# Sums of squares from row-major copies on ScalarE, query projections ahead of the first keys and values, stores on ScalarE's queue, and the memory's norm ahead of the prompt attention

## The chip, the cores and the metric

The kernel runs on one core of a Trainium2 chip. The metric is the device time of one execution in microseconds (us); of several executions the median is given. TensorE is called PE, VectorE DVE, ScalarE ACT, GpSimd POOL and SyncE SP. The kernel is written in a tile framework: its scheduler puts the instructions of each engine in a fixed order, and each engine then works through its own order, waiting where an operand or a buffer isn't ready.

## What is computed

One step of a decoder layer on a prompt of 512 tokens and 8 single sample tokens, all in fp32 with D = 1024. Cut to what matters here:

```python
def rmsnorm(x, g):
    return x * lax.rsqrt(jnp.mean(x * x, axis=-1, keepdims=True) + EPS) * g

def mixer_inputs(x, g_mix, w_in):
    z = rmsnorm(x, g_mix) @ w_in
    return u, q, kv, gates

def mem_project(mem, g_mem, w_xkv):
    return rmsnorm(mem, g_mem) @ w_xkv

def decoder_layer(h, ...):
    u, q, kv, gates = mixer_inputs(h, g_mix, w_in)
    y = concat(pool_mix(u), nsa(q, kv, gates))
    h = h + y @ w_out
    h = h + cross_attn(rmsnorm(h, g_xattn), mem_kv)
    return h + conv_ffn(rmsnorm(h, g_ffn))
```

`nsa` is attention with three branches (compressed blocks, selected blocks, a window) and gates; the sample tokens attend to a paged cache of keys and values. `pool_mix` takes trailing means of 2, 4, 8 or 16 positions minus the token, times a matrix per group. `mem_kv` are keys and values of 256 memory tokens.

## The kernel before

**Data and products.** Activations lie transposed, channels on the partitions: eight blocks (k = 0 to 7) of 128 channels by 520 tokens, in two halves of 260 columns. Each fp32 operand of a projection is split into a rounded high part and the rest (`split`, lines 124 to 129: ACT copies the high part, DVE subtracts), and three products (high x high, high x low, low x high) are added in PSUM. A projection tile of 128 output channels (`project`, line 204) is therefore 8 x 3 x 2 = 48 matmuls of 260 columns. Weights come by DMA into a ring of two buffers ("w_raw"); `split_w` turns them into `w_hi` (ACT, line 117) and `w_lo` (DVE, line 120), two buffers each. Since the weight has to be split before the first product of its tile, ACT's and DVE's order decides when PE may begin a tile.

**The norm.** The products use x times its gain (`xn_hi`, `xn_lo`), and the factor 1/rms of a token is multiplied in afterwards, when the result leaves PSUM (`R1`, `R1n`). Tokens lie along the columns, so the sum of squares over channels is one over partitions: `x_block` (346 to 358) squares each block (six on ACT, two on POOL), POOL and DVE add the squares up in two accumulators, and `token_sums` (from 246) adds over the partitions by small products with a column of ones (lines 255 and 257). `rstd_from` (L213 to L227) is a chain of 13 small DVE operations, `spread_rstd` (L233 to L239) transposes it by PE and copies it to `R`.

**The front.** A few products with a zero tile (L315) come first. Then the first two tiles of keys and values (`ps_kv0`) are projected together, block by block as x arrives. Query tile 0 follows in two banks of its own (`ps_q0`). Then `merge(kv_first, q_tiles)` interleaves two streams by the costs that they yield: `kv_first` multiplies the first keys and values by R1 into `ztile` (a ring of three), stores them (`O["kv_t"]`, L464, SP's queue), rearranges them into `xp_raw` and compresses them by eight small products per tile (L580), then transposes (L595, L478). `q_tiles` projects query tiles 1 to 3 and copies each into `Qst`, `Qbd` and `Qe`. The weights of query tiles 2 and 3 (`load_in` in `q_tiles`) are asked for after the stores. The gate tile (L541) with `turn_queries` (L611) comes next, then `kv_tiles(1)` with the scores of the cached keys (`cached_scores`, L628, L635), then `kv_tiles(2)` and nine steps of `pooling` with `sample_back`, then `sample_attention` with 18 more steps of `pooling`.

**Cached keys.** `fetch_keys` brings one sample's eight pages: of even samples by gathers from POOL (L333), of odd ones by SP (L331), 128 KB each.

**The seam.** After the sample tokens' attention the last steps of `pooling` (the rest of its projection and, for each of four groups, U, POOL's adds in `pl_s`, `pl_d` (L938) and a product with `wpl` (L954) that is split into `y_hi` and `y_lo`) run beside `split_keys`. Then PSUM is given out anew (`ps2`, `ps3`), and `merge(prompt_attention, beside)` starts: `prompt_attention` makes scores (L1002), masked and raised to powers by DVE and ACT (L1008, L1010), transposes (L1031) and weighted sums; `beside` runs `memory` (from 1094), which splits the memory tokens into `mT_hi` and `mT_lo`, squares them on ACT, adds the squares on POOL (`accm`, L1106), sums by ones (L1112), takes rstd, transposes it (L1118), and then projects the memory's keys and values (L1132).

## Time and profile before

| | |
|---|---|
| median of 3 runs | 899.33 us (898.23 to 901.22) |
| the profiled execution | 901.21 us, span 899.1 us |
| mean granted TensorE clock | 0.974 of full speed |
| PE busy | 857.2 us (95%) |
| weight loads (PEld) | 789.3 us (88%) |
| DVE busy | 567.5 us (63%) |
| ACT busy | 369.6 us (41%) |
| POOL busy | 121.6 us (14%) |
| moved by DMA | 122.84 MB, 137 GB/s mean |
| chain of waits | PE 85%, DVE 6%, DMA 4%, ACT 2% |

The busy time is the time of an engine with an instruction in it; a matmul at a low clock is busy as well, only longer. The chain of waits follows the last instruction back to whatever released it. 2.1 us of the profiled execution's time lie outside the span.

### The profile page before, as it was taken

The numbers are of one execution on the slowest core, as the hardware profiler recorded it, in microseconds if no ns is written. First come the engines' busy times: TensorE is split into PE (matmuls) and PEld (weight loads), VectorE is DVE, ScalarE is ACT, GpSimd is POOL, SyncE is SP. The second block draws the span as 40 slices with busy tenths as digits, with TensorE's granted clock in tenths as the row PEclk, the third lists the DMA queues.
The fourth block names the chain that finished last, engine by engine and source line by source line (L and its number), as shares of the span: only waits on it lengthen the run. The fifth ranks groups of instructions, "written<-read, shape, count | busy, mean of one in ns | idle before, by whom it ended". The sixth has DMA issues, their size and how long they took to land.

```text
span 899.1 us, 17462 instructions
## 1 busy us (share of the span) xinstructions
PE 857.2 (95%) x7085; PEld 789.3 (88%) x7085; DVE 567.5 (63%) x1450; ACT 369.6 (41%) x684; POOL 121.6 (14%) x114
## 2 busy tenths in 40 slices
PE   7989999699999999999999999999999999999993
PEld 6978786587777789999889999999999999999993
DVE  6653173987665767788764578773377774367734
ACT  5432132566656546344343254441144442134541
POOL 6713033400000004000043000000000000000132
PEclk9988999979999999999999999999999999999995
DMA  8943795342332146477514643322333322332212
GB/s 281 322 153 107 269 354 199 117 154 97 106 118 71 47 132 213 143 236 250 179 47 118 230 137 98 94 93 83 87 84 85 90 94 94 95 94 84 81 36 95
DMA packets 108175, 122.84 MB, mean 137 GB/s; under 512 B 4592, under 2 KB 95088, under 8 KB 106032
## 3 DMA queue, kind: packets, MB, share of 16 engines
q1 hardware_dynamic: 103488, 100.79, 35.5%
q0 software_dynamic: 3600, 19.55, 5.9%
q10 hardware_dynamic: 1008, 1.40, 0.4%
q8 instruction: 55, 0.90, 0.4%
q14 instruction: 24, 0.20, 0.1%
HBM read 114.58 MB, written 10.69 MB: 139 GB/s over the span
## 4 chain that ended last, share of the span: by engine, by line
PE 85%; DVE 6%; DMA 4%; ACT 2%; issue 1%; SPq 0%; DVEq 0%; ACTq 0%; POOL 0%; POOLq 0%
PE ps_pp L204 56%; PE ps_tb L1132 3%; PE ps_sc L1002 3%; DMA w_u<-in_w_up_dram 3%; PE ps_o L1038 2%; PE ps_tb L1153 2%; PE ps_tb L973 2%; PE ps_tf L1031 2%; PE ps_pp L1604 2%; DVE w_lo L120 1%; PE ps_x L1322 1%; PE ps_x L1341 1%; ACT w_hi L117 1%; PE ps_s L1379 1%; DMA w_kv<-in_w_in_t_dram 1%
## 5 line engine op out<-in xcount | busy, mean ns | idle before, releaser
L204 PE MATMUL ps_pp<-x_hi,w_lo 128*128 128x260 f32 x832 | 169.2, 284 | 0.5 <-DVE w_lo L120 0.5
L204 PE MATMUL ps_pp<-x_hi,w_hi 128*128 128x260 f32 x832 | 169.5, 284 | 0.1
L204 PE MATMUL ps_pp<-x_lo,w_hi 128*128 128x260 f32 x832 | 167.8, 283 | 0.0
L204 PEld LDWEIGHTS ps_pp<-x_hi,w_lo 128*128 128x128 f32 x832 | 128.7, 188 | 1.2 <-DVE w_lo L120 0.7
L204 PEld LDWEIGHTS ps_pp<-x_hi,w_hi 128*128 128x128 f32 x832 | 128.7, 188 | 0.5 <-ACT w_hi L117 0.3
L204 PEld LDWEIGHTS ps_pp<-x_lo,w_hi 128*128 128x128 f32 x832 | 128.1, 188 | 0.4 <-issue 0.4
L117 ACT ACTIVATE w_hi<-w_raw 128x1024 fp32r<-128x1024 f32 (+1 forms) x52 | 54.2, 1043 | 107.6 <-PE ps_pp L204 85.9
L120 DVE TENSOR_TENSOR hT<-hT,ps_pp 128x520 f32<-128x520 f32 (+1 forms) x44 | 28.4, 646 | 88.6 <-PE ps_pp L204 74.5
L117 ACT ACTIVATE w_hi<-w_u 128x1024 fp32r<-128x1024 f32 x44 | 46.7, 1061 | 76.0 <-PE ps_pp L204 65.0
L120 DVE TENSOR_TENSOR w_lo<-w_raw,w_hi 128x1024 fp32r<-128x1024 f32 (+1 forms) x52 | 64.5, 1241 | 4.3 <-ACT w_hi L117 4.0
L204 PE MATMUL ps_pp<-h_lo,w_hi 128*128 128x260 f32 x304 | 61.3, 283 | 0.0
L204 PE MATMUL ps_pp<-h_hi,w_hi 128*128 128x260 f32 x304 | 61.2, 282 | 0.0
L204 PE MATMUL ps_pp<-h_hi,w_lo 128*128 128x260 f32 x304 | 61.1, 282 | 0.0
L120 DVE TENSOR_TENSOR ext<-ps_pp,R 128x512 f32<-128x512 f32 x44 | 30.4, 690 | 45.4 <-PE ps_pp L204 45.3
L120 DVE TENSOR_TENSOR w_lo<-w_u,w_hi 128x1024 fp32r<-128x1024 f32 x44 | 53.9, 1226 | 7.0 <-ACT w_hi L117 6.7
L204 PE MATMUL ps_pp<-xn_hi,w_hi 128*128 128x260 f32 x208 | 48.8, 316 | 5.0 <-ACT w_hi L117 2.9
L1551 POOL DMA_DIRECT2D out_ffn_t_dram<-last x1 | 0.6, 574 | 351.1 <-DVE last L114 351.1
L204 PE MATMUL ps_pp<-xn_lo,w_hi 128*128 128x260 f32 x208 | 46.5, 304 | 0.8 <-DVE xn_lo L129 0.7
L204 PEld LDWEIGHTS ps_pp<-h_hi,w_hi 128*128 128x128 f32 x304 | 46.9, 188 | 0.2 <-ACT h_hi L117 0.2
L204 PEld LDWEIGHTS ps_pp<-h_hi,w_lo 128*128 128x128 f32 x304 | 46.9, 188 | 0.0
L204 PEld LDWEIGHTS ps_pp<-h_lo,w_hi 128*128 128x128 f32 x304 | 46.8, 188 | 0.0
L204 PE MATMUL ps_pp<-xn_hi,w_lo 128*128 128x260 f32 x208 | 45.7, 302 | 0.3 <-DVE w_lo L120 0.3
(457 smaller groups left out, 1884.3 us busy)
## 6 DMA issues: line engine op xcount, KB each, us to landing
w_u<-in_w_up_dram SPq DMA_DIRECT2D x44, 512.0 KB, 4.6
xkr<-in_cache_mem_dram SPq DMA_DIRECT2D x16, 512.0 KB, 5.1
xvr<-in_cache_mem_dram SPq DMA_DIRECT2D x16, 512.0 KB, 6.2
w_raw<-in_w_down_dram SPq DMA_DIRECT2D x8, 1024.0 KB, 5.2
Kt<-in_k_t_dram SPq DMA_DIRECT2D x32, 128.0 KB, 4.0
w_raw<-in_w_in_t_dram SPq DMA_DIRECT2D x8, 512.0 KB, 4.3
w_raw<-in_w_xkv_dram SPq DMA_DIRECT2D x4, 1024.0 KB, 5.4
w_v<-in_w_xkv_dram SPq DMA_DIRECT2D x4, 1024.0 KB, 5.1
```

Source lines behind the costliest of these rows:

```text
L117: act.activation(o, i, AF.Copy, scale=scale)
L120: (eng or dve).tensor_tensor(o, a, b, op=op)
L204: pe.matmul(o, a[:, k, :], x[:, hf, :], start=(k == 0 and j == 0), stop=(k == kt - 1 and j == 2))
L973: pe.matmul(ps[:, :HT], a[:, k, :], y[x][:, k, hf, :], start=(k + j == 0), stop=(k == 3 and j == 2))
L1002: pe.matmul(ss_[hl][:, 0:c0 + nk], Qst[:, h, qc], k[:, g, u, 0:c0 + nk], start=(u == 0), stop=(u == 1))
L1031: pe.transpose(pt[:, hh * P:(hh + 1) * P], pr[hh][:, kb * P:(kb + 1) * P], ident)
L1038: pe.matmul(po[hp * 64:(hp + 1) * 64, g * 256:(g + 1) * 256], Vtok[:, br, kb - 1, g * 64:(g + 1) * 64], pTs[kb - 1][:, hp * 256:(hp + 1) * ...
L1132: pe.matmul(ps[:, 0:MEM], a[:, k, :], x[:, k, :], start=(k == 0 and j == 0), stop=(k == 7 and j == 2))
L1153: pe.matmul(ps[i], x[:, k, ts_], w[:, kl, :], start=(k == 0 and j == 0), stop=(k == KT - 1 and j == 2))
L1322: pe.matmul(s[:, ql * MEM:(ql + 1) * MEM], a[:, 2 * h + dh, hf, ql * P:(ql + 1) * P], x[:, 2 * h + dh, :], start=(n == 0), stop=(n == 5))
L1341: pe.matmul(po, v[:, mb, dh * P:(dh + 1) * P], x[:, mb, :], start=(mb + j == 0), stop=(mb + j == 3))
L1604: pe.matmul(ps[:, l, :HT], a[:, dl, k, :], x[:, hf, :], start=(k + j == 0), stop=(k == kt - 1 and j == 2))
```

## The change

It does five things. (1) The host gives x and the memory tokens a second time in their natural layout, tokens on the partitions (`x_row`, `x_row_s`, `mem_row`); ACT squares a row of 1024 channels and sums it in the same instruction (`accum_out`), one for each 128 tokens. The squares of the transposed blocks, their sums on POOL and DVE and the products with ones go. (2) There are 16 products with the zero tile where there were 6. (3) The query tiles run alone, directly after tile 0; `kv_begin` makes the first keys' two `ztile`s ahead of them; compression, gate and `turn_queries` are merged after them; the weights of query tiles 2 and 3 and some keys are fetched earlier; the sample's first scores and the window's scores run beside `kv_tiles(1)`, and all 27 steps of `pooling` are beside `sample_attention`. (4) The stores of keys and values go out on ACT's queue. (5) `memory_norm` takes the memory's rstd before `sample_attention`; `memory` keeps the splits and the projections. The two sides of PSUM after the seam are exchanged, and one bank of the prompt attention is taken earlier.

```diff
-    for i in range(6):
+    for i in range(10):
         pe.matmul(pw, warm[:, 0:P], warm, start=True, stop=True)
...
     def x_block(k):
         split(xn_hi[:, k], xn_lo[:, k], hT[:, k], scale=vec[:, k:k + 1])
-        if k == 0:
-            act.activation(accs[k], hT[:, k], AF.Square)
...
-    raw_q0 = load_in(4, "w_q")
+    raw_q0 = ptile(wp, [P, 2, KT, P], "w_raw", bufs=2, name="w_q")
+    sp.dma_start(raw_q0[:, 0], w_in[4])
+    for i in range(NQB):
+        sp.dma_start(xrow[:, i], A["x_row"][i])
+    sp.dma_start(xrow_s, A["x_row_s"])
+    sp.dma_start(raw_q0[:, 1], w_in[5])
...
+        if k == 1:
+            for _ in range(6):
+                pe.matmul(pw, warm[:, 0:P], warm, start=True, stop=True)
...
     w = split_w(raw_q0[:, 0])
+    ss1 = ptile(rp, [P, 8], "ss", bufs=2)
+    dve.memset(ss1, float(D))
+    for i in range(NQB + 1):
+        n = P if i < NQB else NB
+        act.activation(ptile(px0, [P, D], "xsq")[0:n], xrow[:, i] if i < NQB else xrow_s, AF.Square,
+                       accum_out=ss1[0:n, i:i + 1])
     with tc.high_priority():
-        rs1 = rstd_from(token_sums(bank("s"), *accs), 5)
+        rs1 = rstd_from(ss1[:, 0:5], 5)
...
+    raw_q1 = load_in(6, "w_q")
+    fetch_keys(2)
+    fetch_keys(3)
     wc_raw = ptile(wp, [P, 2, 8, 2, 64], "w_raw", bufs=2, name="wc_raw")
     for c in range(2):
         sp.dma_start(wc_raw[:, c], A["w_cmp_t"][:, c])
-    fetch_keys(2)
-    fetch_keys(3)
+    fetch_keys(4)
+    fetch_keys(5)
...
+    def kv_begin():
+        for c in range(2):
+            z0.append(ztile())
+            tt(z0[c], ps_kv0[c][:, :, :HT], R1, OP.mult)
...
-            sp.dma_start(O["kv_t"][c], z)
+            act.dma_start(O["kv_t"][c], z)
...
-            sp.dma_start(O["kv_t"][2 * br + c], z)
+            act.dma_start(O["kv_t"][2 * br + c], z)
...
+    def sample_front():
+        yield from cached_scores(0)
+        fetch_keys(7)
+        fetch_window_keys()
+        fetch_window_values(0)
+        yield 3.0
+        yield from window_scores()
...
+        pos[2] = bank("o")
...
+    def memory_norm():
+        mrow = ptile(wp, [P, 2, D], "w_raw", bufs=2, name="mrow")
+        sp.dma_start(mrow, A["mem_row"])
+        ssm = ptile(rp, [P, 8], "ss", bufs=2)
+        for i in range(2):
+            act.activation(ptile(pb, [P, D], "wv", name="msq"), mrow[:, i], AF.Square, accum_out=ssm[:, i:i + 1])
+        vcopy(rsm, rstd_from(ssm[:, 0:2], 2))
+        ps = bank("tb")
+        for i in range(2):
+            pe.transpose(ps[:, i * P:(i + 1) * P], rsm[:, i:i + 1].to_broadcast([P, P]), ident)
+        acopy(Rm, ps[:, 0:MEM])
...
-    merge((kv_first(), 10.8), (q_tiles(), 17.0))
-    gates = gate_tile()
-    merge((gates, 4.0), (turn_queries(), 3.0))
+    kv_begin()
+    run(q_tiles())
+    w_g = ptile(p0, [P, KT, 24], "w_g")
+    sp.dma_start(w_g, A["w_gate_t"])
+    raw_kv = [load_in(10)]
+    merge((kv_first(), 4.0), (gate_tile(w_g), 4.0), (turn_queries(), 3.0))
+    raw_kv.append(load_in(12))
     fetch_keys(6)
-    merge((kv_tiles(1), 12.0), (cached_scores(0, 4.0), 10.0))
...
-    merge((ahead(), 18.0), (sample_back(), 24.0))
+    merge((kv_tiles(1, raw_kv[0]), 12.0), (sample_front(), 12.0))
+    merge((kv_tiles(2, raw_kv[1]), 12.0), (sample_back(), 12.0))
...
-    merge((sample_attention(), 20.0), ((next(pools) for _ in range(18)), 12.0))
+    memory_norm()
+    pools = pooling()
+    merge((sample_attention(), 20.0), ((next(pools) for _ in range(27)), 19.0))
...
-    es_ps2 = open_psum("ps2", "right", tb=3)
-    es_ps3 = open_psum("ps3", "left", sc=2, tf=2, o=1)
+    es_ps2 = open_psum("ps2", "left", tb=3)
+    es_ps3 = open_psum("ps3", "right", o=1, sc=2, tf=2)
```

The scheduler puts all 16 zero products first on PE. Its order on ACT changes most at the front. Before, from the last block of x to the weights of query tile 2 (`xn_hi` and `sqx` belong to x, `w_q` are the query weights, `xp_raw` and `Qst` the rearranged keys and the queries):

```order
L128 ACTIVATE xn_hi<-x_71,vec 128x520
L358 ACTIVATE sqx<-x_71 128x520
L117 ACTIVATE w_hi<-w_q 128x1024 x2
L117 ACTIVATE R<-ps_s 128x2x256 x2
L117 ACTIVATE xp_raw<-ztile 64x32x8 x4
L117 ACTIVATE Qst<-ztile 64x512 x2
L117 ACTIVATE pe_t<-ps_s 64x1
```

The same stretch of ACT after, from the last blocks of x:

```order
L128 ACTIVATE xn_hi<-x_71,vec 128x520 x4
L388 ACTIVATE xsq,ss<-xrow 128x1024 x3
L117 ACTIVATE w_hi<-w_q 128x1024
L388 ACTIVATE xsq,ss<-xrow 128x1024
L388 ACTIVATE xsq,ss<-xrow_s 8x1024
L117 ACTIVATE w_hi<-w_q 128x1024
L117 ACTIVATE R<-ps_s 128x2x256 x2
L479 DMA out_kv_t_dram<-ztile 128x520
L117 ACTIVATE xp_raw<-ztile 64x32x8 x2
L479 DMA out_kv_t_dram<-ztile 128x520
L117 ACTIVATE Qst<-ztile 64x512 x2
L117 ACTIVATE xp_raw<-ztile 64x32x8 x2
```

The squares now stand between the blocks of x and the weights of query tile 0, three ahead of its `w_hi`; the two rows that follow are `Qst` of tile 1 and only then `w_hi` of query tiles 2 and 3.

On PE the seam changes. Before (`accm` are the memory's sums, `ps_sc` scores of the prompt, `ps_tf` their transposes, the last three rows the first of the memory's projection):

```order
L954 MATMUL ps_pp<-pl_d,wpl 128x260 x8
L1002 MATMUL ps_sc<-Ksl,Qst 128x416 x4
L1112 MATMUL ps_tb<-ones,accm 128x1 x2
L1002 MATMUL ps_sc<-Ksl,Qst 128x416 x12
L1031 MATMUL ps_tf<-cst,prob 128x128 x8
L1002 MATMUL ps_sc<-Kwn,Qst 128x384 x2
L1118 MATMUL ps_tb<-cst,rs_y 128x128 x2
L1132 MATMUL ps_tb<-mT_hi,w_hi 128x256
L1132 MATMUL ps_tb<-mT_lo,w_hi 128x256
L1132 MATMUL ps_tb<-mT_hi,w_lo 128x256
```

After:

```order
L969 MATMUL ps_pp<-pl_d,wpl 128x260 x8
L1017 MATMUL ps_sc<-Ksl,Qst 128x416 x4
L1139 MATMUL ps_tb<-mT_hi,w_hi 128x256
L1139 MATMUL ps_tb<-mT_lo,w_hi 128x256
L1139 MATMUL ps_tb<-mT_hi,w_lo 128x256
```

The memory's projection follows directly on the first four scores; twelve scores, the transposes and the rest are spread through it, 24 projection products apart. Ahead of both pieces stand 40 products of the pooling's projection after the sample's last transposes (`oS`), where there were 30.

## Rows read from the trace of the kernel before

**Rows 1.** The page, busy time: us (share of the span) x instructions.

```profile
PE 857.2 (95%) x7085; PEld 789.3 (88%) x7085; DVE 567.5 (63%) x1450; ACT 369.6 (41%) x684; POOL 121.6 (14%) x114
```

**Rows 2.** Windows: length, busy us of each engine (x), TensorE clock, DMA share, GB/s.

```profile
20.00:30.00 10.00, 9.24 (x74) 8.57 (x74) 7.88 (x23) 2.01 (x2) 7.87 (x8) 1.00 0.93 304
...
71.00:78.00 7.00, 7.00 (x33) 6.53 (x32) 2.76 (x11) 0.92 (x3) 5.49 (x5) 0.52 0.57 200
...
161.00:189.60 28.60, 19.44 (x82) 14.93 (x80) 25.82 (x92) 15.53 (x39) 7.66 (x10) 0.78 0.48 150
...
600.00:700.00 100.00, 100.00 (x835) 100.00 (x834) 56.54 (x107) 32.27 (x42) 0.00 (x0) 1.00 0.34 96
```

**Rows 3.** PE's waits from 0 to 240 us: us in total, times, longest.

```profile
PE ps_pp L954 <- DVE y_lo L129: 2.9, 1, 2.9
...
PE ps_tb L595 <- DVE kcp L575: 2.4, 1, 2.4
...
PE ps_pp L954 <- DVE U L120: 1.9, 1, 1.9
...
PE ps_tb L1112 <- POOL accm L120: 2.1, 1, 2.1
...
PE ps_tb L812 <- DVE oS L114: 1.7, 1, 1.7
...
PE ps_tb L819 <- DVE Swn L857: 0.7, 1, 0.7
```

**Rows 4.** Timeline of PE, the front: start, us, instruction, count [idle before <-releaser].

```profile
23.33 1.62 PE L255 MATMUL ps_s<-ones,acc 128*128 128x1 f32 x14
...
26.88 0.40 PE L204 MATMUL ps_pp<-xn_hi,w_lo 128*128 128x260 f32 x2
...
35.15 0.40 PE L204 MATMUL ps_pp<-xn_hi,w_hi 128*128 128x260 f32 x2
...
42.66 1.90 PE L580 MATMUL ps_s<-xp_raw,wc_raw 128*128 128x66 f32 x16
...
49.58 0.80 PE L204 MATMUL ps_pp<-xn_hi,w_hi 128*128 128x260 f32 x2 [2.07 <-ACT w_hi L117]
...
53.99 0.40 PE L204 MATMUL ps_pp<-xn_hi,w_hi 128*128 128x260 f32 x2
...
63.12 0.40 PE L204 MATMUL ps_pp<-xn_hi,w_lo 128*128 128x260 f32 x2
```

**Rows 5.** Timeline of ACT, same columns.

```profile
8.86 0.63 ACT L117 ACTIVATE w_hi<-w_kv 128x512 fp32r<-128x512 f32 x1 [1.84 <-DMA w_kv<-in_w_in_t_dram]
...
36.10 1.28 ACT L117 ACTIVATE Qst<-ztile 64x512 fp32r<-64x512 f32 x2 [0.96 <-DVE ztile L120]
...
48.48 2.00 ACT L117 ACTIVATE w_hi<-w_q 128x1024 fp32r<-128x1024 f32 x2
...
126.34 1.16 ACT L719 ACTIVATE Ssl<-Ssl,mc 128x1025 f32<-128x1025 f32 x1 [1.47 <-DVE mc L718]
```

**Rows 6.** DMA view from 0 to 70 us: GB/s in 40 equal slices.

```profile
GB/s 0 260 346 273 393 411 399 414 249 181 289 183 234 269 309 391 351 298 283 300 295 395 373 352 310 254 277 411 288 14 220 376 293 0 9 0 5 0 0 0
```

**Rows 7.** Timeline of POOL's queue, a gather of keys.

```profile
18.15 1.42 POOL L333 DMA_INDIRECT Kt<-in_k_t_dram,ix_k  x1 [0.19 <-issue]
```

**Rows 8.** Timeline of DVE, the front and the seam.

```profile
27.50 1.22 DVE L120 TENSOR_TENSOR w_lo<-w_q,w_hi 128x1024 fp32r<-128x1024 f32 x1
...
161.78 0.69 DVE L938 SCALAR_TENSOR_TENSOR pl_d<-pl_s,U 128x512 f32<-128x512 f32 x1
...
170.76 1.21 DVE L938 SCALAR_TENSOR_TENSOR pl_d<-pl_s,U 128x512 f32<-128x512 f32 x1
```

**Rows 9.** Timeline of SP's queue, the first stores of keys.

```profile
32.36 0.95 SPq L464 DMA_DIRECT2D out_kv_t_dram<-ztile  x2
```

**Rows 10.** Timeline of PE, the seam.

```profile
166.65 1.04 PE L954 MATMUL ps_pp<-pl_d,wpl 128*128 128x260 f32 x4
...
173.57 3.59 PE L954 MATMUL ps_pp<-pl_d,wpl 128*128 128x260 f32 x8 [2.90 <-DVE y_lo L129]
```

More of the change, by code (lines that the diff above doesn't have):

```diff
@@ L153, in decoder_step @@
     hT = ptile(px0, [P, KT, 2, HT], "x0")
+    xrow = ptile(px0, [P, NQB, D], "xrow")
+    xrow_s = ptile(px0, [NB, D], "xrow_s")
     vec = const.tile([P, 76], F32, name="vec")
@@ L318, in decoder_step @@
     xs1 = blocks(xn_hi, xn_lo)
-    accs = [ptile(px0, [P, 2, HT], f"acc{i}") for i in range(2)]
     def row_numbers():
@@ L408, in decoder_step @@
     Vtok = ptile(at, [P, 2, NQB, P], "Vtok")
+    rsm = ptile(at, [P, 2], "rsm")
+    Rm = ptile(at, [P, MEM], "Rm")
     smp, es_smp = open_pool("smp")
@@ L454, in dup_split @@
         vcopy(lo[b], lo[a].bitcast(F32))
+    z0 = []
+    def kv_begin():
+        for c in range(2):
+            z0.append(ztile())
+            tt(z0[c], ps_kv0[c][:, :, :HT], R1, OP.mult)
     def kv_first():
-        z0 = [ztile(), ztile()]
-        for c in range(2):
-            tt(z0[c], ps_kv0[c][:, :, :HT], R1, OP.mult)
         for c in range(2):
             z = z0[c]
-            sp.dma_start(O["kv_t"][c], z)
+            act.dma_start(O["kv_t"][c], z)
             x = ptile(p0, [P, 528], "chg", bufs=2, name="xp_raw").rearrange("p (j x) -> p j x", j=8)
@@ L501, in q_tiles @@
         for j in range(2):
-            raw = raw_q0 if j == 0 else load_in(4 + 2 * j, "w_q")
-            if j == 1:
-                fetch_keys(4)
-                fetch_keys(5)
+            raw = (raw_q0, raw_q1)[j]
             for l in range(2):
@@ L1022, in weighted @@
         def weighted(qb, br, g, pr):
-            if br + g == 0:
+            if br + g == 0 and qb not in pos:
                 pos[qb] = bank("o")
@@ L1158, in memory @@
             pool.dma_start(mv_out[:, :, cs], Vx[:, :, cs])
-    merge((kv_first(), 10.8), (q_tiles(), 17.0))
-    gates = gate_tile()
-    merge((gates, 4.0), (turn_queries(), 3.0))
-    fetch_keys(6)
-    merge((kv_tiles(1), 12.0), (cached_scores(0, 4.0), 10.0))
-    fetch_keys(7)
-    fetch_window_keys()
-    fetch_window_values(0)
-    pools = pooling()
-    def ahead():
-        yield from kv_tiles(2)
-        for _ in range(9):
-            yield next(pools)
-    merge((ahead(), 18.0), (sample_back(), 24.0))
+    kv_begin()
[5 more added lines that the diff above has]
+    raw_kv.append(load_in(12))
+    fetch_keys(6)
+    merge((kv_tiles(1, raw_kv[0]), 12.0), (sample_front(), 12.0))
+    merge((kv_tiles(2, raw_kv[1]), 12.0), (sample_back(), 12.0))
     es_p0.close()
     pb, es_pb = open_pool("pb")
-    merge((sample_attention(), 20.0), ((next(pools) for _ in range(18)), 12.0))
+    memory_norm()
+    pools = pooling()
+    merge((sample_attention(), 20.0), ((next(pools) for _ in range(27)), 19.0))
     es_pb.close()
@@ L1635, in lay_out @@
     given["x_t"] = np.concatenate([xp, xs], axis=3)
+    given["x_row"] = x["x_prompt"][0].reshape(NQB, P, D)
+    given["x_row_s"] = x["x_sample"][:, 0]
+    given["mem_row"] = x["mem_prompt"][0].reshape(2, P, D).transpose(1, 0, 2)
     given["w_in_t"] = x["w_in"][0][:, :1792].reshape(KT, P, 14, P).transpose(2, 1, 0, 3)
```

49 lines of the change are left out of this document (8 added, 41 removed).

## The prediction

> **What bounds the kernel now.** I read the page's busy times first: PE is at work in 857.2 of 899.1 us, 95%, and no other engine is above 63% [rows 1]. In the middle of the program a window of 100 us has PE busy for all of it at full clock (1.00, the 2.4 GHz level) [rows 2]. So nothing is to be had there, and the change touches nothing behind the seam but order. What can be had is where PE waits, where it runs at the low clock level (1.2 GHz), and products that go. The windows say where: from 161.0 to 189.6 PE is busy 19.4 of 28.6 us at a mean clock of 0.78, and from 71 to 78 the clock is 0.52 with PE busy throughout [rows 2]. The list of PE's waits gives names, nearly all of them ACT's and DVE's chains at the front and the seam [rows 3]. The timeline gives the price of a product: from 53.99 to 63.12 are 76 of them, 0.12 us each; from 49.58 to 53.99, after two waits of 2.4 and 2.1 us, are 18, 0.245 each, so a fall of the level there costs 2.2 us [rows 3, 4].
>
> **The change, part by part** (times of the profiled execution, 901.2 us).
>
> *A. First keys and values, -7.0.* Before, they end at 27.2 (the last two products start at 26.88) [rows 4]. The second weights' first half lands at 8.86 and is split by 9.4 [rows 5]; 6 of 96 products can run ahead of that, and 90 x 0.12 = 10.8 then give 20.2. For that the level must be high from there: 16 zero products keep PE at work from 1.5 until about 8, where six left it idle before the first block. The products with ones, 14 of them in 1.62 us in one piece [rows 4], go; so do POOL's sums, beside which DVE's operations are longer. Bounds: -4 if the level comes as late as before (most of 28 products at twice the price, 3 us back), -8.5 if the waits within go too.
>
> *B. Query tile 0, +1.1.* It took 27.2 to 35.15 = 7.95 [rows 4]. Now its `w_hi` stands on ACT behind three squares of row-major x. The third row block is behind 2.1 MB of x, 1.05 of first weights, 0.5 of `w_q` and 1.6 of itself, 5.3 MB by the tiles' sizes; at 260 to 411 GB/s in the early slices, 304 from 20 to 30 us [rows 2, 6], I let it land at 19.5. One square 1.16 (priced by the nearest, an exponential of 1,025 elements with a sum), `w_hi` 1.0, `w_lo` 1.2 [rows 5, 8]: the second part of the first block runs at 22.9, then 44 products, 5.3, and the six small ones for R, 0.9: 29.2, or 9.0 after A's end. The other two squares and the rstd chain run beside this tile. Bounds 0 (rows land by 18) and +4 (by 22.3).
>
> *C. Query tiles 1 to 3, -1.0.* Before, 35.15 to 63.35 = 28.2, with 3.8 of compression in it (two pieces of 1.90 [rows 4]), which moves behind. The other 24.4 were 17.3 of products, two waits of 4.4, the 2.2 of low level and 0.5. Now tile 2's `w_hi` is queued on ACT behind both copies of tile 1's `Qst`, which wait for tile 1's end: `ztile` 0.7, `Qst` 1.28, `w_hi` 1.0 [rows 5, 8], and `w_lo` still 0.7 after the four products that don't need it; 3.9 in all. With the same fall of the level that saves 0.5, without it 2.7; I take 1.0, nearer the first, since the waits of before were about as long [rows 3]. The weights of tiles 2 and 3 are fetched ahead of most keys and should land by 36. The new query-first order leaves nothing beside these tiles to fill a wait.
>
> *D. Compression, turned queries and cached scores, +2.0.* They follow each other as small products with copies by ACT and DVE between, with only the gate's 32 products beside. A stretch of that kind stood at 0.52 from 71 to 78 and lost 3.3 us [rows 2]. Bounds 0 (this replaces that stretch) and +5.
>
> *E. Middle, +0.3.* The memory's norm puts two squares (1.16 each) on ACT and 14 small operations on DVE, and PE's transposes wait for them: I put 1.0, while the wait on `Swn`, 0.7 [rows 3], gets other work before it. Bounds 0 and +2.
>
> *F. Seam, -7.4.* 19.4 us busy at 0.78 is some 15.2 at full clock. The product with ones and the transposes, about 1, go; ten projection products come, 1.2: 15.4. Of the waits, `oS` 1.7 stays; `U` 1.9 and `y_lo` 2.9 [rows 3] lose about 1.7, since DVE's `pl_d` took 1.21 beside POOL's adds of `accm` and 0.69 without [rows 8], and two or three more operations lie alike; `accm`, 2.1, goes. That makes 15.4 + 1.7 + 3.1 = 20.2, with one fall of the level, 2.2, 22.4 against 28.6; the ten products are missing elsewhere, 1.2 more: -7.4. Bounds -2 and -10.5. Behind `wpl`'s products, which cost 0.26 each at the high level and 0.45 in the low [rows 10], dense projection follows at once instead of twelve scores that wait for DVE each time.
>
> *G. The rest, +0.5.* The two sides of PSUM change places, so the first tiles after the prompt attention lie on banks freed last: 0.5, between 0 and 1.5. The stores held SP for 0.95 [rows 9] with the query weights queued behind; on ACT they hold that engine as long, ahead of `xp_raw` and `Qst`, and ACT isn't busy there. The loads are now issued ahead of the stores anyway: nothing either way.
>
> Sum: -7.0 + 1.1 - 1.0 + 2.0 + 0.3 - 7.4 + 0.5 = -11.5, so 889.7 for the profiled execution. That one lies 1.9 above the median of 899.33: **887.8**.
>
> **The rivals.**
>
> *R1. The seam keeps its waits (about 893).* U, `y_lo` and the fall of the level are one chain through ACT and DVE, and PE has only four scores beside it. If the level stays low for as long as it did, F gives 2 and not 7.4. For it: U and `y_lo`, 4.8 us, are waits that the change doesn't touch itself [rows 3]. Against: what waited for `accm` and what ran between is gone from the order.
>
> *R2. The copies and the gathers share the DMA engines (about 893).* POOL has no squares left, so its gathers of keys, 128 KB in 1.42 us (some 90 GB/s), start when the page numbers are there, near 10.5, and not at 18.15 [rows 7]; 2.1 MB of x are added to the same time, in a stretch whose DMA share was already 0.93 [rows 2]. If the gathers take 90 GB/s from SP's stream for ten microseconds, a third of its rate, the third row block lands at 22.3 and the query weights two to three later: B +2.8, C +2.4, 892.9. For it: 304 GB/s with both at work [rows 2], no more than the 260 to 411 of SP alone [rows 6]. Against: the copies have long rows, and slices with long rows were at 390 to 411. The Trainium skill (DMA: Bandwidth & Descriptors, "Queues, rings and completion order") has each DMA engine take turns between the queues that have work, packet by packet; by that rule this rival holds and SP's stream gives up its share as soon as the gathers begin.
>
> *R3. More than the sum (about 882).* A at -8.5, D at 0.5 and F at -10.5: the level holds from the zero products on, and at the seam it falls only for the products with `wpl`.
>
> *R4. Slower (about 904).* With the query tiles alone, nothing fills PE's wait before tile 2. If the level falls there and stays down until the gate is through, tiles 2 and 3 cost 96 x 0.12 = 11.5 more, of which 2.2 are counted, the small products some 3.3 more and the gate 3.8 more: 887.8 + 16.4 = 904.2. It decides from some 120 products at the low level on. Against: in the same place before, the level was back after 18 products [rows 4]; for: from 71 to 78 it stayed down with PE busy throughout [rows 2].
>
> **How the numbers follow.** A measurement of this kernel can tell about 0.3%, 2.7 us, from no change. The sum with its neighbours, 883.5 to 892: 0.46. R3: 0.15. R1: 0.13. R2: 0.14. Half of A and F given back together, 896.6 to 902.0: 0.06. R4 and its like: 0.06. Faster by over 0.3% is the first four, 0.88; within 0.3% 0.06; slower 0.06. The range goes from 879, most of R3, to 895.5, most of R1 and R2, and leaves out some 0.19.
>
> **What would show it.** A: the first keys and values end by 20 to 21 with products 0.12 us apart from 9.4 on. B: ACT waits for `xrow`, and PE's wait before query tile 0 is 1 to 2.5 us. C: one wait of 3 to 4 us on `w_hi` before tile 2, the level back within 20 products. D: the gate ends by 63 to 66. F: PE's waits on `accm` are gone, those on U and `y_lo` below 4 together, and the first memory projection stands 8 to 11 us ahead of 189.6, counted from what the front gained. The prediction is wrong if query tile 0 waits beyond 24 us, if the clock is low over more than one tile at the front, or if waits of more than 3 us appear between 100 and 160 us, where 27 steps of pooling now lie beside one phase and none beside the one ahead.

## The result, and the profile after

The changed kernel takes **894.46 us** (892.46 to 897.30) where the kernel before takes 899.33 (898.23 to 901.22), five executions of each: a ratio of 0.9946, 95% interval 0.9923 to 0.9969. It is faster, by 4.9 us and not by the 11.5 of the forecast. The time lies in the range, near its upper end. The profiled execution took 897.3 us (span 895.5), 2.8 above its median; that of before lay 1.9 above its own, so the two spans differ by 3.6 only, and the accounts below are of that 3.6.

The page of the changed kernel, busy time and the chain of waits by engine, against [rows 1]:

```profile
PE 853.9 (95%) x7073; PEld 788.4 (88%) x7073; DVE 560.6 (63%) x1444; ACT 371.2 (41%) x684; POOL 112.1 (13%) x102
...
PE 84%; DVE 6%; DMA 6%; ACT 2%; issue 1%; SPq 0%; DVEq 0%; POOL 0%; ACTq 0%; POOLq 0%
```

PE is busy 3.3 us less, and DMA's part of the chain went from 4% to 6%. Where PE waits, in the list for 0 to 240 us (us in total, times, longest), against [rows 3]:

```profile
PE ps_pp L206 <- ACT w_hi L117: 5.1, 2, 3.2
PE ps_s L235 <- DVE rs_y L229: 3.7, 1, 3.7
PE ps_s L658 <- DMA Wk<-in_win_k_t_dram: 2.8, 1, 2.8
PE ps_sc L1017 <- DVE y_lo L129: 2.1, 1, 2.1
PE ps_tb L827 <- DVE oS L114: 2.0, 1, 2.0
PE ps_pp L969 <- DVE y_lo L129: 1.8, 2, 1.7
...
PE ps_tb L1119 <- DVE rsm L114: 1.1, 1, 1.1
```

`kcp`, `U` and `accm` are gone from it. The second row, the fourth and the last are new: PE waits for the chain of 1/rms inside query tile 0, for `y_lo` ahead of the first scores, and for the memory's norm. The timeline of PE at the front, against [rows 4], shows where:

```profile
20.41 0.40 PE L206 MATMUL ps_pp<-xn_hi,w_lo 128*128 128x260 f32 x2
21.02 0.51 PE L206 MATMUL ps_tb<-xn_hi,w_hi 128*128 128x260 f32 x2 [0.20 <-ACT w_hi L117]
...
30.64 1.11 PE L235 MATMUL ps_s<-cst,rs_y 128*128 128x128 f32 x4 [3.66 <-DVE rs_y L229]
...
33.89 0.64 PE L206 MATMUL ps_pp<-xn_hi,w_hi 128*128 128x260 f32 x2
...
43.89 0.80 PE L206 MATMUL ps_pp<-xn_hi,w_hi 128*128 128x260 f32 x2 [3.19 <-ACT w_hi L117]
...
49.60 0.40 PE L206 MATMUL ps_pp<-xn_hi,w_hi 128*128 128x260 f32 x2
...
58.23 2.57 PE L589 MATMUL ps_s<-xp_raw,wc_raw 128*128 128x66 f32 x22
```

The first keys and values end at 20.65 (before: 27.2). Query tile 0 then takes 13.24 us, to 33.89: the clock falls with the wait of 3.66 and stays down until 35.99. From there to 58.23 PE does tiles 1 to 3, with a second wait and a second fall of the level, which is back at 49.60. The cause of the wait of 3.66 stands on ACT, DVE and POOL. First ACT's square of the fourth row block and DVE's rows of the changed kernel, then POOL's, the first of them from the kernel before:

```profile
23.02 1.06 ACT L388 ACTIVATE xsq<-xrow 128x1024 f32<-128x1024 f32 x1 [2.06 <-DMA xrow<-in_x_row_dram]
```

```profile
25.39 1.87 DVE L215 TENSOR_SCALAR rs_ms<-ss 128x5 f32<-128x5 f32 x1 [3.17 <-ACT xsq L388]
...
28.48 1.23 DVE L120 TENSOR_TENSOR w_lo<-w_q,w_hi 128x1024 fp32r<-128x1024 f32 x1
...
30.42 0.17 DVE L229 SCALAR_TENSOR_TENSOR rs_y<-rs_t,rs_y 128x5 f32<-128x5 f32 x1
```

```profile
1.21 1.82 POOL L432 MEMSET QW<- 128x2064 f32 x1
...
21.22 1.82 POOL L334 DMA_INDIRECT Kt<-in_k_t_dram,ix_k  x1 [0.30 <-issue]
25.42 1.82 POOL L439 MEMSET QW<- 128x2064 f32 x1 [2.38 <-ACT xsq L388]
27.39 0.95 POOL L334 DMA_INDIRECT Kt<-in_k_t_dram,ix_k  x1 [0.15 <-issue]
```

ACT waits for the fourth row block until 23.02 (the third was there at 18.71) and has squared the sample tokens at 25.35. The chain's first operation, 128 x 5 numbers, then takes 1.87 us: it runs to the same moment as POOL's clearing of `QW`, a zeroed matrix of 1 MB. Before, POOL cleared it at 1.21 us. Now it waits for ACT's squares (2.38) and starts with the chain: `QW` lies in memory of the pool that the copies and their squares use first, and in the run without the copies, below, the clearing is back at 1.22. The Trainium skill (SBUF — State Buffer, "SBUF: two separate sides") says that POOL's instructions and some kinds of DVE's compete for one pair of ports, which the one that starts first keeps to its end while the other stands. The two rows end together (27.26 and 27.24), as by that rule; their starts (25.39 and 25.42) are too close to tell which came first. And in the middle of the chain stands `w_lo` of tile 0's second part, 1.23.

The seam, PE, against [rows 10]:

```profile
164.25 0.33 PE L827 MATMUL ps_tb<-cst,oS 128*128 128x128 f32 x1 [2.04 <-DVE oS L114]
...
174.61 1.14 PE L969 MATMUL ps_pp<-pl_d,wpl 128*128 128x260 f32 x4 [1.66 <-DVE y_lo L129]
...
179.19 1.74 PE L1017 MATMUL ps_sc<-Ksl,Qst 128*128 128x416 f32 x4 [2.11 <-DVE y_lo L129]
180.73 0.41 PE L1139 MATMUL ps_tb<-mT_hi,w_hi 128*128 128x256 f32 x1
```

The memory's projection begins at 180.73 instead of 189.59. The windows of the changed kernel (columns as in [rows 2]) give the rest:

```profile
20.65:33.90 13.25, 8.87 (x57) 7.94 (x56) 7.69 (x23) 4.94 (x9) 9.20 (x8) 0.82 0.88 221
33.90:58.20 24.30, 21.09 (x145) 20.58 (x145) 12.57 (x30) 8.41 (x12) 12.49 (x12) 0.82 0.84 265
58.20:72.10 13.90, 13.73 (x174) 12.63 (x172) 7.41 (x26) 5.71 (x21) 2.84 (x3) 0.68 0.53 185
...
100.00:110.00 10.00, 10.00 (x163) 7.46 (x166) 0.07 (x1) 0.60 (x1) 0.94 (x1) 0.79 0.98 347
```

Compression and turned queries run at a mean clock of 0.68; term D had gone by a stretch of 0.52. From 100 to 110, behind a wait of 2.8 on `Wk`, the mean clock is 0.79, where before it was 1.00.

### The profile page after: what moved, and what is told of

Read it like the earlier page. It is cut to its first block, busy times and chain, and to the rows that moved or that the text cites. A ratio compares the mean times of both kernels' runs of the same rounds, so it can differ in the third digit from the quotient of the medians.

```text
span 895.5 us, 17406 instructions
## 1 busy us (share of the span) xinstructions
PE 853.9 (95%) x7073; PEld 788.4 (88%) x7073; DVE 560.6 (63%) x1444; ACT 371.2 (41%) x684; POOL 112.1 (13%) x102
## 3 DMA queue, kind: packets, MB, share of 16 engines
q0 software_dynamic: 3600, 19.55, 6.1%
## 4 chain that ended last, share of the span: by engine, by line
PE 84%; DVE 6%; DMA 6%; ACT 2%; issue 1%; SPq 0%; DVEq 0%; POOL 0%; ACTq 0%; POOLq 0%
PE ps_pp L206 57%; PE ps_tb L1139 3%; PE ps_tb L1160 3%; DMA w_u<-in_w_up_dram 3%; PE ps_o L1053 2%; PE ps_sc L1017 2%; PE ps_tb L988 2%; PE ps_pp L1606 2%; PE ps_tf L1046 2%; DMA xrow<-in_x_row_dram 1%; PE ps_x L1343 1%; PE ps_x L1324 1%; DVE w_lo L120 1%; PE ps_s L1381 1%; DMA Wk<-in_win_k_t_dram 1%
## 5 line engine op out<-in xcount | busy, mean ns | idle before, releaser
L206 PEld LDWEIGHTS ps_pp<-xn_hi,w_hi 128*128 128x128 f32 x208 | 34.7, 203 | 11.4 <-ACT w_hi L117 5.5
```

Of the source, the lines that this page charges most:

```text
L206: pe.matmul(o, a[:, k, :], x[:, hf, :], start=(k == 0 and j == 0), stop=(k == kt - 1 and j == 2))
```

## The experiments

**Two kinds of chip.** The runs fell on several chips, of two kinds by the time of the kernel before: 899 us on the first kind (the result above, and the fourth group of runs) and 935 to 938 on the second (four chips, one for each of the other groups). Every ratio below is against the kernel before on the same chip. On the second kind the changed kernel gains 15 us (919.96 for 935.15), and this was the first surprise. It ran unchanged on one chip of that kind only, that of the second group; where runs of another group are set against its 0.9834, the comparison goes from chip to chip.

**First group: which of the causes at tile 0?** All four start from the changed kernel. The first moves POOL's clearing:

```diff
-    pool.memset(QW, 0.0)
...
     fetch_keys(4)
     fetch_keys(5)
+    pool.memset(QW, 0.0)
```

> The changed kernel, with POOL's clearing of QW written behind the gathers of keys. Theory T (the sums end late): in the changed kernel DVE's first operation on the sums took 1.87 us beside this clearing, and the chain behind it held PE 3.66 us before the transposes of 1/rms, after which 16 products or so ran at the low level. Moved away, that operation takes 0.2, PE's wait there falls to about 1.9, and the time falls by 1.7, or by 3.5 if the level stays up: 891 to 893 for 894.5. Rival S (traffic: the copies and gathers push the weights back): the weights land as before, no change beyond 0.5 us.

Measured: 0.983 (0.9795 to 0.9866). The chain's first operation took 0.44 and PE's wait on `rs_y` was gone, but PE waited 11.95 us ahead of tile 0: with no clearing between them, 16 gathers of keys ran in one piece and the weights of tile 0 landed behind them. The row on DVE fits the theory; that PE no longer waits for the chain does not show it, since PE had waited elsewhere, and the price could not be read there.

The next two take the squares from transposed x: with the copies loaded and unused, and without them.

```diff
-        act.activation(ptile(px0, [P, D], "xsq")[0:n], xrow[:, i] if i < NQB else xrow_s, AF.Square,
+        act.activation(ptile(px0, [P, D], "xsq")[0:n], hsq[:, i % NQB] if i < NQB else hsq[0:NB, 0], AF.Square,
```

> The changed kernel, with ScalarE's five squares reading blocks of the transposed x, which lies there already, in place of the row-major copies; these are still loaded. The sums are others, so the outputs are not the reference's. T: the squares no longer wait for the third and fourth row block, the chain ends by 25, no wait before the transposes of 1/rms, the level stays up, query tile 1 begins near 28 where it began at 33.9: 4 to 6 us faster, 888.5 to 890.5. S: the query weights still land late behind the copies, and PE waits for them instead: under 2 us faster, 892.5 or more.

> As the run before, and without the loads of the row-major x (2.1 MB less in the first 25 us). The outputs are not the reference's. T: within 1.5 us of the run before, since then no engine waits for what stands behind these copies. S: 3 us or more faster than the run before.

Measured: 0.9777 (0.9744 to 0.9809) and 0.9849 (0.982 to 0.9878). With squares that need not wait for the copies the wait on `rs_y` goes; with 2.1 MB fewer to load the kernel was slower, since POOL then ran its 24 gathers in one piece and PE waited 14.3, 5.6 and 4.0 us. Whether the bytes of the copies cost anything can't be told from this pair, since the order of the gathers changed with them.

The fourth puts the two sides of PSUM back:

```diff
-    es_ps2 = open_psum("ps2", "left", tb=3)
-    es_ps3 = open_psum("ps3", "right", o=1, sc=2, tf=2)
+    es_ps2 = open_psum("ps2", "right", tb=3)
+    es_ps3 = open_psum("ps3", "left", sc=2, tf=2, o=1)
```

> The changed kernel, with the two sides of PSUM after the seam put back as before (memory's banks on the right, the prompt attention's on the left). Theory P: the first scores, and the memory's projection behind them, waited 2.1 us for the last y_lo in the changed kernel only because the exchange put their bank on one of the last pooling product; put back, this wait falls to below 0.5 and the time by 1 to 2 us, 892.5 to 893.5. Rival: the wait is the same chain in another place (PE has nothing else to do), and the time doesn't change by more than 0.7; or the exchange was worth something later, and it is slower by 1 or more.

Measured: 0.9796 (0.9763 to 0.9829). PE's timeline of this run at the seam:

```profile
201.65 1.31 PE L1017 MATMUL ps_sc<-Ksl,Qst 128*128 128x416 f32 x4
204.12 0.39 PE L1139 MATMUL ps_tb<-mT_hi,w_hi 128*128 128x256 f32 x1 [1.16 <-DVE y_lo L129]
```

The scores no longer wait; the projection behind them waits 1.16 on the same `y_lo`. By these rows (1.16 for 2.11, on two chips) the exchange of sides cost about 1 us, inside the bounds of term G (0 to 1.5); the time can't show it, for 0.9796 and the changed kernel's 0.9834 there have intervals that overlap.

**Second and third group: why does the second kind gain more?** The changed kernel again, and the kernel before with a trace:

> The changed kernel as it is, so that the next three can be set against it on the same chip. Its ratio to before was 0.9946 (0.9923 to 0.9969). If the front's transfers decide what it gains, as the four runs before suggest, whose chip took 938 us for the kernel before and where PE stood still for 12 us in a piece at the front, the ratio on another chip may be further from 1 than that interval: 0.975 to 0.995.

> The kernel before, unchanged, for its trace on this chip. If the chip is like that of the first result: 898 to 901 and no pieces without a named cause. If it is like that of the eight runs above (932 to 941): PE stands still in pieces of 5 to 15 us at the front while POOL's gathers run, and transfers of SyncE's queue land only as the gathers end.

Measured: 0.9834 (0.9808 to 0.986) and 0.9995 (0.9972 to 1.0018). PE's largest waits at the front, the kernel before on a chip of the second kind, with ACT's split of the weights that it waits for, then the changed one:

```profile
50.75 1.06 ACT L117 ACTIVATE w_hi<-w_q 128x1024 fp32r<-128x1024 f32 x1 [32.07 <-remote]
...
51.86 0.80 PE L204 MATMUL ps_tb<-xn_hi,w_hi 128*128 128x260 f32 x2 [23.90 <-ACT w_hi L117]
```

```profile
24.35 0.80 PE L206 MATMUL ps_tb<-xn_hi,w_hi 128*128 128x260 f32 x2 [3.90 <-ACT w_hi L117]
...
55.16 0.80 PE L206 MATMUL ps_pp<-xn_hi,w_hi 128*128 128x260 f32 x2 [14.99 <-ACT w_hi L117]
```

And POOL's gathers beside them, the first and the last of 24 in one piece before, and what stands between the first eight and the next sixteen after:

```profile
18.19 1.43 POOL L333 DMA_INDIRECT Kt<-in_k_t_dram,ix_k  x1 [0.18 <-issue]
...
47.99 0.95 POOL L333 DMA_INDIRECT Kt<-in_k_t_dram,ix_k  x1 [0.30 <-issue]
```

```profile
20.90 0.95 POOL L334 DMA_INDIRECT Kt<-in_k_t_dram,ix_k  x1 [0.30 <-issue]
26.58 1.82 POOL L439 MEMSET QW<- 128x2064 f32 x1 [4.74 <-ACT xsq L388]
28.55 0.95 POOL L334 DMA_INDIRECT Kt<-in_k_t_dram,ix_k  x1 [0.15 <-issue]
...
48.92 0.95 POOL L334 DMA_INDIRECT Kt<-in_k_t_dram,ix_k  x1 [0.30 <-issue]
```

Before, the query weights were issued at 9.27, and ACT could split them only at 50.75, when the gathers had ended; "remote" means that the profile doesn't name what ended the wait. After, the eight first gathers end at 21.9, POOL waits for the squares, and in this pause the weights of tile 0 can be split (23.25). Behind tile 1's products the front stands still until the other sixteen gathers have ended, at 49.9: DVE waits 13.0 ("remote") before tile 1's `ztile`, until 52.01, and ACT's `Qst` (52.75) and tile 2's `w_hi` (54.05) follow it. The DMA view of the kernel before on that kind, from 18 to 50 us (mean busy share in 40 slices; SP's queue):

```profile
DMA  9996899978999999857532823415338225135044
...
q1 hardware_dynamic: 2649, 3.32, 34.6%
```

SP's queue moved 3.32 MB there, and 6.96 in the same stretch on the first kind; from 32 us on the engines' mean share is mostly below a half, so it is not the sum of the bytes that holds the loads. On this kind the weights come late while gathers run in one piece, and the late clearing, which costs 1.7 us in the chain, is what splits the gathers. That the gathers are the cause is argued from this order of times, and from a run below in which moving them moved the wait; no run without gathers fell on this kind. By the turns between queues, packet by packet, of the Trainium skill (DMA: Bandwidth & Descriptors, "Queues, rings and completion order"; rival R2), SP's stream should have lost a share; that weights issued at 9.27 could be split only at 50.75 the rule does not tell.

A second thing marks this kind. While gathers run, PE also stands between single products with nothing in the profile to wait for ("issue"), in the changed kernel at the cached scores:

```profile
PE ps_s L637 <- issue: 6.5, 11, 1.0
```

Such waits come to 3.8 us in the kernel before on this kind, to 16.9 and 17.7 in query tiles of runs below, and to none in either kernel on the first kind. Their cause is open, and no run tells how much of the 36 us between the kinds they are.

Four tries to use that, each a change of the order alone. The weights of tiles 2 and 3 ahead, the clearing kept behind eight gathers (run twice); all 24 gathers behind the clearing; the weights ahead and the clearing behind all 24; a buffer of its own for tile 1's `ztile`:

```diff
+    raw_q1 = load_in(6, "w_q")
     sp.dma_start(WT, A["w_cmp_e"])
...
-    raw_q1 = load_in(6, "w_q")
```

> The changed kernel, with the weights of query tiles 2 and 3 asked for ahead of WT and of the first sample's keys on SyncE's queue; nothing else (POOL's order is held). In the changed kernel they were issued at 36.1, because the eight single pages ahead of them took 15.9 us to issue. Theory Q (the wait of 3.2 us ahead of query tile 2, and the fall of the level behind it, come from this load): the wait goes below 0.5, tile 2 follows at the high level, 4 to 5 us less than the changed kernel. Rival (the wait comes from ScalarE's order, Qst of tile 1 ahead of w_hi): the scheduler puts one w_hi ahead here, so the wait goes as well, but if the load's place is what only counts for the scheduler, the gain is the same; they part where ScalarE waits: for Q on a DMA ahead of that w_hi in the changed kernel. Rival S (the DMA engines are full at any order): the first query weights or the rows land later by as much, under 1.5 us less.

> As e6 (the weights of query tiles 2 and 3 asked for ahead of WT and the eight pages). Q, where transfers are as in the first result: 4 to 5 us less than the changed kernel, a ratio of 0.989 to 0.991. On a chip like that of e6: 0.984 to 0.990, no gain over the changed kernel.

```diff
-            fetch_keys(0)
...
     pool.memset(QW, 0.0)
+    fetch_keys(0)
```

> The changed kernel, with POOL's clearing of QW ahead of its gathers, so that none of these runs before 25 us (in the changed kernel eight run from 11.3 to 23). Theory R2 of the prediction (gathers take their share from the row-major copies): the fourth row block lands at about 20 and not at 23, ScalarE's wait on it of 2.1 us goes, the 1/rms chain ends 2 to 3 us earlier, and the eight pages on SyncE's queue take 10 us and not 16, so the query weights come earlier too: 3 to 6 us less than the changed kernel. Rival: the rows land when they do because of their own 2.1 MB: under 1 us.

> As e6, with the clearing of QW behind 24 gathers, so that it no longer runs beside DVE's first operation on the sums. If both T and Q hold: 6 to 8 us less than the changed kernel; T alone 2, Q alone 4.

```diff
-                z = ztile()
+                z = ztile() if x != 1 else ptile(p0, [P, 536], "zq")[:, 0:2 * HT].rearrange("p (r t) -> p r t", r=2)
```

> The changed kernel, with a buffer of its own for query tile 1's result, so that this no longer waits for the first store of keys to be read out of the buffer that it takes over. Theory W: on the chip of e5 that wait, 13 us on DVE, was the store (260 KB on ScalarE's queue, issued at 34, over by 52) and PE's 15 us ahead of tile 2 hung on it: there 8 us or more less than the changed kernel, a ratio near 0.975. Where the store lands in 4 us, as in the first result, nothing: 0.9946 within 0.002. Rival: on that chip the next thing, the weights of tile 2, lands no earlier, and under 3 us are gained.

Measured: 0.9874 (0.9849 to 0.9899) and 0.9857 (0.982 to 0.9893); 0.991 (0.9882 to 0.9937), with one wait of 25.2 at tile 2; 0.9936 (0.9914 to 0.9957); 0.9815 (0.9784 to 0.9845), where the wait of 14.4 on tile 2's weights stayed. None is faster than the changed kernel there by more than the intervals, and the two with 24 gathers in one piece are slowest. The second tells most: with all gathers behind the clearing (24.9 to 55.8), tile 0's weights are split at 19.55 (23.25 in the changed kernel) and the fourth square starts at 20.52 without a wait, but tile 2's weights come only after the gathers' end:

```profile
62.61 0.80 PE L206 MATMUL ps_pp<-xn_hi,w_hi 128*128 128x260 f32 x2 [25.21 <-ACT w_hi L117]
```

Moving the gathers moves the wait. The third shows the other thing: 16.9 us of its front are "issue" waits at tile 0's products, in eight pieces. With early weights tile 3 ended at 61.8, not 69.5, but the wait on `oS` at the seam began 2.5 us later (187.15 for 184.68): 10 us were lost between, and where is not settled (a wait on `Pc` of 3.3 in place of 1.3 is 2.0 of them). The last is a miss for the store as the cause: with a buffer of its own, DVE's `zq` still waits 13.4 ("remote"), until 51.78, and `Qst` and tile 2's `w_hi` stand behind it on ACT. What it waits for stays open. And squares from transposed x once more:

> As e2 (squares from the transposed x, the row-major copies loaded and not used; the outputs are not the reference's), on a chip that may be another. T: where the front's transfers are as in the first result, no wait ahead of the transposes of 1/rms, 4 to 6 us less than the changed kernel, a ratio to before of 0.988 to 0.991. S: over 0.993.

Measured: 0.9766 (0.9734 to 0.9799), below the changed kernel's 0.9834 (0.9808 to 0.986) by 0.7%, on another chip of the second kind. The wait at tile 2 is 3.2 for 15.0, but 9.9 us of "issue" waits stand in the query tiles instead; where the 0.7% come from is not settled.

**Fourth group: no gathers.** The theory was one of the second kind, but these runs fell on the first, so it stays untested. All keys come by SP; in the changed kernel the weights of tiles 2 and 3 are ahead as above.

```diff
-            if b % 2:
+            if True:
```

> The kernel before, with the keys of all eight samples fetched page by page on SyncE's queue, and none gathered by POOL. Theory G (on the chip of the last twelve runs a transfer of SyncE's or ScalarE's queue lands only when POOL's gathers pause): the first query weights, issued at 9.3 and there at 50.8 in the kernel before on that chip, land by 18, and the 23.9 us wait of PE goes; SyncE's longer queue costs some 5 us at query tile 2. 935 to 940 becomes 905 to 915, a ratio of 0.965 to 0.975. Rival (the chip's transfers are slow for another reason, whatever POOL does): 0.99 or more.

> The changed kernel with all keys on SyncE's queue, the weights of query tiles 2 and 3 ahead of them (as in e6) and the compression's weights ahead of the third sample's keys. G with Q: no PE wait at the front over 4 us, 890 to 898 on that chip, a ratio to before of 0.95 to 0.957; on a chip like that of the first result 0.985 to 0.99. Rival (SyncE's 64 page loads of 1 us each are now late for the cached scores at about 65): a new wait of 5 us or more there.

Measured: 1.0128 (1.0101 to 1.0155) and 1.0177 (1.0148 to 1.0206). Both are slower than with gathers, for SP is then the narrow place: in the second, the pages of all eight samples, two at a time, held its queue for 25.3, 18.2, 18.0 and 18.6 us, and `Wk` and what follows were issued at 104 instead of 90; in the first, the load of tile 2's weights was issued only at 51.24, and they made PE wait 9.69. The expectation for the second on this kind, 0.985 to 0.99, was missed. But its front is what the forecast had meant, as ACT's row of the fourth square and PE's timeline show:

```profile
20.65 1.04 ACT L389 ACTIVATE xsq<-xrow 128x1024 f32<-128x1024 f32 x1
```

```profile
28.20 0.65 PE L235 MATMUL ps_s<-cst,rs_y 128*128 128x128 f32 x4 [1.42 <-DVE rs_y L229]
...
30.27 0.51 PE L206 MATMUL ps_pp<-xn_hi,w_hi 128*128 128x260 f32 x2
...
49.37 2.00 PE L618 MATMUL ps_tb<-Qe,WT 64*128 64x64 f32 x16 [1.55 <-DVE Qe L114]
```

The fourth row block is there without a wait 2.4 us earlier than in the changed kernel (20.65 for 23.02), tile 0 takes 9.47 us from its first product (20.80) to tile 1's where that took 12.87, no query tile waits on `w_hi` for more than 0.2, and tile 3 ends at 47.8, ahead of the wait of 1.55, where the changed kernel ends it at 58.23 and the forecast had 52.6 (20.2, 9.0 and 23.4). The loss lies behind, in the window from 120 to 140 us of this kernel:

```profile
120.00:140.00 20.00, 3.77 (x13) 2.56 (x14) 8.94 (x42) 6.80 (x13) 1.57 (x2) 0.50 0.99 398
```

PE is busy 3.8 of 20 us there, against 18.85 in the changed kernel; it waits 8.9 us for the memory's norm, 6.5 for a `w_hi` and 3.7 for `Pc`.

On top of that, `QW` in a pool of its own (cleared at the start), and, on top of the run without that, squares from transposed x:

```diff
-    QW = ptile(p0, [P, 16 * P + 16], "QW")
+    pqw, es_pqw = open_pool("pqw")
+    QW = ptile(pqw, [P, 16 * P + 16], "QW")
```

> As e14, with QW in a pool of its own above the others, so that POOL clears it in the first microseconds and not beside DVE's first operation on the sums. T: that operation takes 0.2 and not 1.9, PE's wait ahead of the transposes of 1/rms is 1.7 shorter, 1.7 to 3.5 us less than e14. Rival: nothing, as the chain still ends with the last row block.

> As e14, with the squares taken from the transposed x (row-major copies loaded and not used; the outputs are not the reference's). T: PE's wait ahead of the transposes goes altogether and the level stays up: 4 to 6 us less than e14. S: under 2.

Measured: 1.0151 (1.0127 to 1.0176), and 1.0179 (1.0152 to 1.0205). The first rows of the chain on DVE, without the pool and with it:

```profile
23.00 1.88 DVE L215 TENSOR_SCALAR rs_ms<-ss 128x5 f32<-128x5 f32 x1 [0.99 <-ACT xsq L389]
```

```profile
22.67 0.17 DVE L215 TENSOR_SCALAR rs_ms<-ss 128x5 f32<-128x5 f32 x1 [0.99 <-ACT xsq L389]
```

1.88 becomes 0.17, PE's wait on `rs_y` goes, and the turned queries start at 47.42, 1.95 us earlier: the cost of the clearing, read by itself (in the times 2.9 us, with intervals that overlap). Tile 1 now begins at 28.33, 7.86 us after tile 0's first product at 20.47:

```profile
28.33 0.51 PE L206 MATMUL ps_pp<-xn_hi,w_hi 128*128 128x260 f32 x2
```

Squares without the copies gave 0.5 us (915.77 for 916.28, with intervals that overlap), where 4 to 6 were expected, and do not price the squares: `QW`'s clearing lay beside the chain's first operation once more (1.87, at 20.23), `w_lo` came only at 23.06, behind seven of the chain's operations on DVE, and PE waited 2.40 for it in tile 0, where the level fell.

**Last group: the clearing and the weights by themselves, gathers in place.** These fell on the second kind.

> The changed kernel with the zeroed matrix QW in a pool of its own, so that it no longer lies on the memory of the row-major copies and POOL can clear it at the start; gathers of keys stay on POOL. Theory T (the 1/rms chain is late because its first DVE operation lies beside POOL's clearing, 1.87 us for 0.17, with the split of w_lo in the middle of the chain): that operation takes under 0.5, PE's wait on rs_y is 1.7 to 2.2 instead of 3.7, tile 1 starts 1.5 to 2 us earlier, and where the kernel before takes 899 the time is 1.5 to 3 us below that of the change. Rival (the chain waits for the rows, and the clearing costs nothing): the wait stays above 3.2 and the time does not move. Where the kernel before takes 935 the gathers lose their pause of six microseconds and the time rises by 3 to 10, as in the runs that moved the clearing there.

> As the run before it, and the query weights of tiles 2 and 3 loaded ahead of the compression's weights and of the second page of keys. Where the kernel before takes 899: their load is issued near 13 to 15 us instead of 36, PE's wait of 3.2 on w_hi ahead of tile 2 falls to 1 to 2 (the copies of tile 1's queries still stand ahead of it on ACT), and the time is 1 to 3 us below that of the run before it. Rival (that wait is ACT's order, not the weights): the wait stays at 3 or more and the time does not move. Where the kernel before takes 935: no gain over the run before it, since the gathers then hold the loads.

Measured: 0.9895 (0.9867 to 0.9924) and 0.9921 (0.9895 to 0.9947). DVE's first operation of the chain is 0.17, as expected, but 24 gathers run without a pause from 10.76, and in the first of the two DVE waits 5.02, until 34.99, for the second half of tile 0's weights in the middle of the chain, while PE stands 17.7 us in ten "issue" waits. So both gain less than the changed kernel did (0.9834, on another chip), as was written for this kind; what they would give on the first kind was not measured.

## Why the prediction was wrong in size

The sign and the range were right, and most of the seam came (5.6 of 6.9); of the 11.5 us, 4.9 came. That the time lies in the range is luck: its upper end was left for R1 and R2, and R1, the seam that keeps its waits, did not come. By the forecast's terms, from the two profiled executions (the marks are the end of the first keys and values, the start of tile 1, the end of tile 3, the start of the wait on `oS`, the end of the products with `w_out`):

| term | forecast | measured | from |
|---|---|---|---|
| A first keys and values | -7.0 | -6.5 | 27.2 to 20.65 |
| B query tile 0 | +1.1 | **+5.3** | 7.95 to 13.24 |
| C tiles 1 to 3 | -1.0 | -0.1 | 24.4 to 24.34 |
| D, E to the seam | +2.3 | +3.6 | 97.8 to 103.98, less 3.8 moved in, plus 1.2 moved out |
| F, G seam | -6.9 | -5.6 | 171.1 to 166.7, less 1.2 moved in |
| later | 0 | -0.2 | 566.8 to 566.6 |
| sum | -11.5 | -3.5 | spans: -3.6 |

- **A was right.** Sixteen zero products did what was written, and the end at 20.65 lies in "20 to 21".
- **B is the step that failed**, in the sentence "The other two squares and the rstd chain run beside this tile". The chain must be over before the tile is, since `R` stands ahead of tile 0's last seven products and of everything that leaves PSUM. I priced the third row block (19.5 forecast, 18.71 measured) and put the fourth, at 23.02, and the chain behind it at nothing. So the tile took 13.24 for 9.0, beyond the bound of +4. The fall of the level that the waits bring is 2 us of this: 13.24 less 6.7 of products at full clock less 0.37, 0.52 and 3.66 of waits. The runs without gathers part the causes. From its first product to tile 1's, tile 0 took 7.67 before (27.48 to 35.15) and takes 12.87 changed, 9.47 without gathers, where the fourth row block is in time, and 7.86 with the clearing moved too. So some 3.4 go with the late row block and 1.6 with the clearing, both with what they bring of the lower level; the first step also changed the order of other loads, and was run on a chip of the first kind that may be another one. `w_lo`, 1.23, stands in the chain in all three kernels, and costs nothing once the others are gone. Nothing in the diff names `QW`; only the memory that its pool got changed. I had read the orders of ACT and PE, not POOL's. PE's wait before the tile, by contrast, was 0.20 and 0.52, not the 1 to 2.5 that I had named as a sign.
- **C**: the wait is there with 3.2 (3.9 forecast, though the parts named add to 3.7), and so is the fall. As forecast, `w_hi` (42.78) stands on ACT right behind `Qst` (41.48 and 1.28 long). But "The weights of tiles 2 and 3 ... should land by 36" was wrong: SP issued them at 36.08, behind eight page loads that held its queue from 15.04 to 30.93, and then a wait of its own for the store of keys on ACT's queue:

```profile
SPq L188 <- DMA out_kv_t_dram<-ztile: 4.1, 1, 4.1
```

So G's "The loads are now issued ahead of the stores anyway" was wrong too; what ties the two is not shown. And in C the level was still low for the first products of tile 1, from 33.89 to 35.99, 1 us, which belongs to B's wait.
- **D and E** came to 3.6 for 2.3 together. Of D only the mean clock can be told, 0.68; the gate ended near 76.6, not at 63 to 66. **E** was too small: `Wk` now makes PE wait 2.8 (before 1.5), the memory's norm 1.1 (forecast 1.0), and from 100 to 110 the clock is 0.79 where it was 1.00.
- **F**: `accm` and `U` are gone, `pl_d` takes 0.69 throughout, `y_lo` 1.66, one fall of the level from 165.4 to 169, and the four scores wait 2.11 on the exchanged PSUM, which G had as 0.5. Up to the memory's first product the seam took 28.6 us (161.0 to 189.6) and takes 18.5 (162.2 to 180.73), but part of that gain is work put off: twelve scores and their transposes now stand behind that mark, and at the end of `w_out` 4.4 are left.
- **The rivals.** R2's mechanism came, one row block later than it had it: the gathers began at 11.33, the third block was not late (18.71, not 22.3), the fourth was, by 2.4 us or more against the run without gathers; tile 0's weights were not late on the first kind of chip. That the time is near R2's 893 has other causes too, the clearing and E. R4 did not come: the level fell twice at the front and was back each time within 24 products.
- **The signs named.** Two of those that were to show the prediction wrong came: tile 0 waited beyond 24 (until 30.64), and the clock was low over two stretches of the front, from 30.64 to 35.99 and from 43.89 to 49.60. The third did not: no wait of more than 3 us from 100 to 160.

## What to carry to other kernels

A sum that is moved off the critical engine onto a later load has two ends: price the last piece of the load and the whole chain behind it, against the first use of its result, and not only the first piece against the engine's queue. When tiles or pools go or change size, look at what gets their memory: an operation that the diff doesn't touch may now wait for the last reader there, as `QW`'s clearing did, beside the one chain that mattered. And look at the front with another chip in mind: the same order gained 0.5% on one and 1.7% on one of another kind, for a reason that no term of the forecast held.

## What had not been expected of the hardware

- On a chip of the second kind, while 24 gathers from POOL ran, 1.25 us apart, query weights loaded by SP's queue were not there to be split until the gathers had ended (issued 9.27, split at 50.75); with all gathers later, the weights of tile 2 came late instead of tile 0's. On the first kind, with the same program and the same gathers, query weights landed 5.0 to 6.9 us after their issue. What differs between the kinds is open.
- A DVE operation of 0.17 us took 1.87 beside POOL's clearing of 128 x 2064 numbers, three times alike (1.87, 1.88, 1.87), and 0.17 where the clearing lay elsewhere.
- The granted clock reads 1.00 from 9.5 to 27.2 in the kernel before, although products there stood 0.216 us apart until 16.4 and 0.12 later; the spacing of the products, not the granted clock, showed the lower level.
